# Modulation loads emitted a step ahead, sums stored later, and the backward scan pass re-cut into one chunk per half projection

## The chip, the cores and the metric

The kernel runs on one core of a Trainium2 chip. A core has a matrix engine (TensorE, PE in the profile, with its weight loads shown as PEld), a vector engine (VectorE, DVE), an activation engine (ScalarE, ACT), GpSimd (POOL) and a sync engine (SyncE, SP) whose queue issues nearly all DMA transfers. PSUM is the memory that matmuls write to, SBUF the one that everything else lives in. The metric is the time of one execution on the device, in microseconds (us). All arithmetic is in 32-bit floats.

## The reference

One layer of a diffusion backbone for 256 prompt tokens and 1024 sample tokens of width 1024, which share all weights. A conditioning vector per group gives shift, scale and gate vectors through one large product (the modulation). The mixer has a short gated convolution and a Mamba-2 scan (SSD) that runs over the tokens in chunks of 128, forward and backward. A gated feed-forward block with a 3x3 convolution follows. Cut to what matters here:

```python
mod_lat = (silu(c) @ w_ada + b_ada).reshape(c.shape[0], 1, N_MOD, D_MODEL)   # and mod_ctx from c_ctx
proj = h @ w_in                                     # hc, gb, gc, z, xbc, dtf, dtb
out_a = gb * dwconv1d(gc * hc, w_conv_short)
xbc = silu(dwconv1d(xbc, w_conv_ssd, b_conv_ssd))   # -> xs, bm (B), cm (C)
dt = softplus(dtf + dt_bias)                        # and the same for dtb
# scan, per chunk of 128 positions and head
da = dt * a;  cs = cumsum(da)                       # within the chunk
chunk_states = einsum('bcshn,bhcs,bcshp->bchpn', b_c, exp(cs[-1] - cs), x * dt)
state = exp(cs[-1]) * state + chunk_states          # from chunk to chunk
y = ((C B^T) * exp(cs_l - cs_s)) @ (x * dt) + exp(cs) * (C @ state_at_start)
```

The backward scan is the same over reversed positions. The prompt starts from zero states and returns its final ones; the sample starts from given states.

## The kernel before, in words

Large products are done as three matmuls in a rounded format (`mm3`): the weight tile is split into a high and a low part, and so is the activation. Lines 166, 168 and 170 issue high x high, high x low and low x high. `wload` loads a weight tile of 512 KB into `raw`, ACT rounds it to the high part (line 157), and DVE or GpSimd subtracts to get the low part (`wlo`). A sample projection has 1024 columns and accumulates in an `acc` tile of PSUM, a prompt projection has 256 and uses `pj`.

Between about 70 and 230 us the kernel makes the eight `xbc` tiles of the scan's input (sample and prompt, function `xbc_both`; "the seventh tile" is the one with i = 7, which is made last), and among them small prompt projections and eight modulation steps (`ada_steps`, a generator advanced by `next(mods)`). A modulation step multiplies eight weight tiles `ws` (128 x 512, eight buffers) with the conditioning vectors (line 186: sixteen matmul instructions in the trace, in two groups of four tiles), copies the result to `ss` and transposes it (line 196). `dtstage` and `dtstage2` turn the raw time steps into `dt`, the sums `cs` and decay factors on DVE and ACT, and store `cs` to DRAM in `csdp` (prompt) and `csds` (sample), from where `ssd_pass2` later broadcasts them over the partitions (`bc`).

The scan has two passes. `ssd_pass1` is the backward one: it goes through the chunks from the last to the first (prompt chunks 1 and 0, sample chunks 7 to 1). For each chunk `tok_major` transposes x (line 576, PSUM tile `xt`) and B (line 579, `bt`), ACT copies `bt` to `btok`, DVE scales `xt` to `xd`. `state_step` then forms the products of `btok` and `xd` (line 594, PSUM tile `ad`), and adds them to the decayed state, which DVE (or ACT by a copy, line 600, for the first) writes to `sb`; the state is stored to DRAM (`sbdp`, `sbds`). All of `xt`, `bt` and `ad` come from three PSUM buffers named `sa`. `ssd_pass2` is the forward pass; its `prep` adds masks to the broadcast sums (`wm`) on DVE and takes exponentials on ACT (line 676).

While the scan runs on small matmuls, PE gets long ones from `fillers`: the z projections and the gated-convolution projections of the sample, each in two halves (`next(filler)` runs one half). In pass 1, two chunks were handled for every z projection.

The order on each engine follows the order in which the code emits instructions, as changed by the scheduler of the framework, which may move an instruction past others that it does not depend on; `after(a, b)` asks for a to come behind b. Each engine then works through its list in order and waits where a semaphore says so; so does SP's queue of transfers.

Of the kernel before, what the change touches and what calls it, by code (L numbers as in the profile page):

```python
# [13 lines left out]
P = 128  # L14
# [4 lines left out]
L = 128  # L19
# [36 lines left out]
def body(nc, tc, A):  # L56
    cnt = [0]

    def T(pool, shape, tag, bufs, dt=F32):
        cnt[0] += 1  # L60
        return pool.tile(list(shape), dt, tag=tag, bufs=bufs, name=f"{tag}_{cnt[0]}")
# [12 lines left out]
    dma = nc.sync.dma_start  # L74
# [37 lines left out]
    sc = T(con, [P, KT, 32], "sc", 1)  # L112
# [12 lines left out]
    g_nrm, nrm = open_pool("nrm")  # L125
# [13 lines left out]
    def psa():  # L139
        return T(ps, [P, 512], "sa", 3)  # L140


    wn, w_dma = [0], [None]
# [30 lines left out]

    def ada_steps():

        for e in range(8):
            pt = psa()
            for k0 in (0, 4):
                ws = [T(nrm, [P, 512], "ws", 8) for _ in range(4)]  # L180
                for q, w in enumerate(ws):
                    d = dma(w, A["w_ada"][(k0 + q) * P:(k0 + q + 1) * P, e * 512:(e + 1) * 512])
                    if k0 == q == 0:
                        after(d, w_dma[0])
                for q in (3, 2, 1, 0):
                    mm = nc.tensor.matmul(pt[32 * q:32 * q + 32, :], sc[:, k0 + q, :], ws[q],
                                          start=k0 == 0, stop=k0 == 4, skip_group_check=True,
                                          tile_position=(0, 32 * q))
                    if k0 == 0 and q == 3:
                        after(mm, mid_mm[0])  # L190
            s = T(nrm, [P, 512], "ss", 2)
            act(s, pt, AF.Copy)
            yield
            tp = psa()
            for b in range(4):
                mm = nc.tensor.transpose(tp[:, b * P:(b + 1) * P], s[:, b * P:(b + 1) * P], ident)
                if b == 0:
                    after(mm, mid_mm[0])
            b0 = 16 + e * 4
            V.tensor_reduce(out=mod[:, b0:b0 + 4, :],  # L200
                            in_=tp.rearrange("p (b g v) -> p b v g", b=4, g=4)[:, :, 0:2, :],
                            axis=mybir.AxisListType.X, op=ALU.add)
            tt(mod[:, b0:b0 + 4, :], mod[:, b0:b0 + 4, :],
               smv("bada")[:, b0:b0 + 4].unsqueeze(2).broadcast_to([P, 4, 2]), ALU.add)
        yield
# [8 lines left out]
    def after(a, b):  # L214

        tc.add_manual_dep(a.ins, b.ins.name, mybir.DependencyInfo(
            mybir.DependencyClass.NoSync, mybir.DependencyReason.DATA), reason="table order")
# [35 lines left out]
    for k in range(KT):  # L253
        dma(xs[k], xT[:, k, TP:TT])
        q = T(cv, [P, TS], "cv", 4)
# [61 lines left out]
    for k in range(KT):  # L317
# [23 lines left out]
        q, i = k // 4, k % 4  # L341
# [11 lines left out]
    for name, t0, n, v in (("p", 0, TP, 0), ("s", TP, TS, 1)):  # L353
        s = S()
# [5 lines left out]
    SP, SS = sets  # L360
# [3 lines left out]
    last_mm, mid_mm = [], [None]  # L364
# [6 lines left out]
    def xbc_both(i, order, lo_eng):  # L371

        wh, wl = wload(A["w_in"][16 + i], lo_eng, raw_b())
        for s in order:
            small = s.name == "p"
            pp = pj() if small else pacc()
            outs = [(pp[:, a:b], (lambda k, a=a, b=b: s.hi(k)[:, a:b]), (lambda k, a=a, b=b: s.lo(k)[:, a:b]))
                    for a, b in s.chunks]
            ks = list(range(KT))
            for half in [ks] if small else [ks[0:KT // 2], ks[KT // 2:]]:  # L380
                ends = mm3(outs, wh, wl, KT, half)
                mid_mm[0] = ends[0]
                last_mm.append(ends[-1])
                if half[-1] < KT - 1:
                    yield
            conv_x(s, i, pp[:, 0:s.T], s.xbc[i])
        yield
# [103 lines left out]
    def dtstage(s, d4):  # L491
        n = s.T
        v = T(cv, [40, n], "cv", 4)
        for a, b in s.chunks:
            p2 = psa()
            mm = nc.tensor.matmul(p2[0:40, 0:b - a], sel, d4[:, a:b], start=True, stop=True)
            if a == 0:
                after(mm, last_mm[-1])
            vi = act(v[:, a:b], p2[0:40, 0:b - a], AF.Identity, bias=rows[:, 1:2])
        u = T(cv, [40, n], "cv", 4)  # L500
        stt(u, v, -1.0, v, ALU.mult, ALU.min)
        ex = act(u, u, AF.Exp)
        if s.name == "p":
            after(ex, lnexp_table(vi))
        w = T(cv, [40, n], "cv", 4)
        V.tensor_scalar(out=w, in0=u, scalar1=1.0, scalar2=None, op0=ALU.add)
        lw = T(cv, [40, n], "cv", 4)
        act(lw, w, AF.Ln)
        stt(u, w, -1.0, u, ALU.add, ALU.subtract)
        act(w, lw, AF.Exp, scale=-1.0)  # L510
        tt(u, u, w, ALU.mult)
        tt(lw, lw, u, ALU.subtract)
        stt(v, v, 0.0, lw, ALU.max, ALU.add)
        da = u
        V.tensor_scalar(out=da, in0=v, scalar1=arow, scalar2=None, op0=ALU.mult)
        rm = w
        rm3 = rm.rearrange("p (c l) -> p c l", l=L)
        V.memset(rm, 1.0)
        V.memset(rm3[0:32, :, 0:1], 0.0)
        V.memset(rm3[32:40, :, L - 1:L], 0.0)  # L520
        cs = lw
        V.tensor_tensor_scan(out=cs, data0=rm, data1=da, initial=0.0, op0=ALU.mult, op1=ALU.add)
        V.tensor_tensor_scan(out=cs[32:40, ::-1], data0=rm[32:40, ::-1], data1=da[32:40, ::-1],
                             initial=0.0, op0=ALU.mult, op1=ALU.add)
        for a in range(2):
            for g in range(2):
                r = 32 * a + 4 * g
                dma(s.csd[:, g, a].rearrange("c h l -> h c l"),
                    cs[r:r + 4, :].rearrange("h (c l) -> h c l", l=L))
        return v, u, cs  # L530

    def dtstage2(s, v, u, cs):
        V.tensor_scalar(out=v, in0=v, scalar1=1e-37, scalar2=None, op0=ALU.max)
        act(v, v, AF.Ln)
        tt(v, v, cs, ALU.subtract)
        ce = T(sd, [40, s.nc], f"ce{s.name}", 1)
        cs3 = cs.rearrange("p (c l) -> p c l", l=L)
        V.tensor_copy(ce[0:32, :], cs3[0:32, :, L - 1])
        V.tensor_copy(ce[32:40, :], cs3[32:40, :, 0])
        e2 = u  # L540
        tt(e2.rearrange("p (c l) -> p c l", l=L), v.rearrange("p (c l) -> p c l", l=L),
           ce.unsqueeze(2).broadcast_to([40, s.nc, L]), ALU.add)
        act(e2, e2, AF.Exp)
        return v, e2, ce

    def dttok(s, v, e2, ce):
# [201 lines left out]
    g_nrm, nrm = open_pool("nrm2")  # L748
# [24 lines left out]
    mods = ada_steps()  # L773
    for i, n in zip(range(N_LOOP, 7), (2, 2, 2, 4, 4)):
        for t in range(n):
            next(small)
            if t == 0 and i >= 4:
                next(mods)
        if i == 2:
            dts = dtstage2(SP, *dtstage(SP, d4_p))  # L780
        if i == 4:
            early[0] = False
            bcs = [T(sd, [P, TS], "bcs", 4) for _ in range(4)]
            SS.B, SS.C = bcs[0:2], bcs[2:4]
            SS.xbc += bcs
        both = xbc_both(i, (SS, SP), PG if i < 4 else PV)
        next(both)
        if i > 2:
            next(mods)
        if i == 4:  # L790
            dttok(SS, *dts)
        next(both)
        if i == 2:
            dttok(SP, *dts)
            dts = dtstage(SS, d4_s)
        if i == 3:
            dts = dtstage2(SS, *dts)
        if i == 4:
            after(act(xall, xall, AF.Silu), SS.last_exp)
            for k in range(4):  # L800
                silu_s(k)
        if i >= 4:
            silu_s(i)
        if i == 5:
            act(bcall[:, 0:2], bcall[:, 0:2], AF.Silu)
# [19 lines left out]
    filler = fillers()  # L825
# [7 lines left out]
    def pairs(scan):  # L833
        return [(step, c, copies(c)) for copies, step, c in scan]

    def steps(cps, behind):
        for (step, c, cp), b in zip(cps, behind):
            step(c, cp, b)

    scan = ssd_pass1(SP)  # L840
    both = xbc_both(7, (SP, SS), PV)
    cps = pairs(scan[0:1])
    next(both)
    cps += pairs(scan[1:2])
    next(both)
    act(bcall[:, 2:4], bcall[:, 2:4], AF.Silu)
    silu_s(7)
    steps(cps, (last_mm[-2], last_mm[-1]))
    close_pool(g_ps)
    g_ps, ps = open_pool("ps3", space=PSUM)  # L850
    ph_p[0] = False
    scan = ssd_pass1(SS)
    for i in range(0, len(scan), 2):
        cps = pairs(scan[i:i + 2])
        next(filler)
        mid_mm[0] = last_mm[-1]
        next(filler)
        steps(cps, (last_mm[-2], last_mm[-1]))

    def gate(x, c0, n):  # L860

# [332 lines left out]
    for blk in range(2):  # L1194
        steps = norm2_b_steps() if blk == 0 else final_steps(0, OA)
# [125 lines left out]
```

## Time and profile before

| | |
|---|---|
| time, median of 3 runs | 1573.53 us (1571.55 to 1574.64) |
| the profiled execution's own time | 1575.05 us |
| its span, first to last instruction | 1572.7 us |
| mean granted TensorE clock | 0.990 |
| PE busy | 1524.0 us, 97% of the span |
| DVE busy | 1094.2 us, 70% |
| ACT busy | 653.2 us, 42% |
| HBM traffic | 163.70 MB read, 22.63 MB written |

A row of the timeline reads: start in us, length in us, engine, line of the code, operation, tile written <- tiles read, shape, number of instructions merged; in brackets the idle time of the engine ahead of it and who ended it. Tile names are without their buffer numbers. "SPq" rows are transfers being issued by SP's queue, not their landing. The granted clock is the share of full speed that the clock throttle left to PE.

### The profile page before, as it was taken

The numbers are of one execution on the slowest core, as the hardware profiler recorded it, in microseconds if no ns is written. First come the engines' busy times: TensorE is split into PE (matmuls) and PEld (weight loads), VectorE is DVE, ScalarE is ACT, GpSimd is POOL, SyncE is SP. The second block draws the span as 40 slices with busy tenths as digits, with TensorE's granted clock in tenths as the row PEclk, the third lists the DMA queues.
The fourth block names the chain that finished last, engine by engine and source line by source line (L and its number), as shares of the span: only waits on it lengthen the run. The fifth ranks groups of instructions, "written<-read, shape, count | busy, mean of one in ns | idle before, by whom it ended". The sixth has DMA issues, their size and how long they took to land. (4 is left out here: it accounts for less than half of the span.)

```text
span 1572.7 us, 22526 instructions
## 1 busy us (share of the span) xinstructions
PE 1524.0 (97%) x8722; PEld 1297.4 (82%) x8722; DVE 1094.2 (70%) x1628; ACT 653.2 (42%) x1019; POOL 519.3 (33%) x289
## 2 busy tenths in 40 slices
PE   6999998999999999999999999999999999999997
PEld 2577886787788888888888888888888888888886
DVE  4764354258886448896666597656679878798696
ACT  6444434157786335433322353222344433433333
POOL 0431331111111001434333333333346545455452
PEclk9999999999999999999999999999999999999999
DMA  8445653344434613221222242222243333343321
GB/s 296 157 159 177 216 197 128 110 150 145 141 110 164 254 55 112 82 76 66 78 73 68 66 146 92 73 69 66 95 164 104 92 107 99 101 156 98 94 78 61
DMA packets 90652, 187.79 MB, mean 119 GB/s; under 512 B 9746, under 2 KB 37298, under 8 KB 90546
## 3 DMA queue, kind: packets, MB, share of 16 engines
q1 hardware_dynamic: 84722, 183.22, 34.8%
q10 hardware_dynamic: 5824, 3.15, 0.7%
q8 instruction: 68, 1.11, 0.3%
q14 instruction: 38, 0.31, 0.1%
HBM read 163.70 MB, written 22.63 MB: 118 GB/s over the span
## 5 line engine op out<-in xcount | busy, mean ns | idle before, releaser
L80 DVE SCALAR_TENSOR_TENSOR cc<-acc,sm,cc 128x504 f32<-128x504 f32 (+5 forms) x836 | 545.9, 665 | 111.2 <-ACT cc L1061 52.3
L77 POOL TENSOR_TENSOR wlo<-raw,whi 128x1024 fp32r<-128x1024 f32 (+2 forms) x91 | 214.7, 2359 | 652.3 <-ACT whi L157 608.7
L157 ACT ACTIVATE whi<-raw 128x1024 fp32r<-128x1024 f32 x97 | 102.6, 1057 | 250.1 <-PE acc L168 211.9
L80 DVE SCALAR_TENSOR_TENSOR x<-dn,mod,x 128x288 f32<-128x288 f32 (+2 forms) x176 | 96.1, 547 | 95.2 <-PE dn L170 94.5
L77 POOL TENSOR_TENSOR dlo<-draw,dhi 128x512 fp32r<-128x512 f32 (+1 forms) x88 | 108.9, 1238 | 91.1 <-ACT dhi L1114 91.1
L77 POOL TENSOR_TENSOR wlx<-raw,whx 128x1024 fp32r<-128x1024 f32 (+2 forms) x36 | 83.5, 2320 | 147.2 <-ACT whx L157 131.4
L168 PE MATMUL acc<-ya,whi 128*128 128x512 f32 (+1 forms) x400 | 118.7, 354 | 0.0
L166 PE MATMUL acc<-ya,whi 128*128 128x512 f32 (+1 forms) x400 | 118.7, 354 | 0.0
L170 PE MATMUL acc<-ya,wlo 128*128 128x512 f32 (+1 forms) x400 | 118.6, 354 | 0.0
L170 PE MATMUL acc<-oa,wlo 128*128 128x512 f32 (+1 forms) x400 | 118.5, 354 | 0.0
L168 PE MATMUL acc<-oa,whi 128*128 128x512 f32 (+1 forms) x400 | 118.5, 353 | 0.0
L166 PE MATMUL acc<-oa,whi 128*128 128x512 f32 (+1 forms) x400 | 118.1, 353 | 0.0
L166 PE MATMUL dn<-yb,dhi 128*128 128x288 f32 (+2 forms) x352 | 110.2, 313 | 5.3 <-DVE x L80 4.1
L168 PE MATMUL dn<-yb,dhi 128*128 128x288 f32 (+2 forms) x352 | 109.6, 311 | 1.1 <-POOL yb L77 1.1
L170 PE MATMUL dn<-yb,dlo 128*128 128x288 f32 (+2 forms) x352 | 109.6, 311 | 0.0
L166 PE MATMUL acc<-h,whi 128*128 128x512 f32 x336 | 109.5, 407 | 0.0
L168 PE MATMUL acc<-h,whi 128*128 128x512 f32 x336 | 106.7, 398 | 0.0
L170 PE MATMUL acc<-h,wlo 128*128 128x512 f32 x336 | 105.9, 397 | 0.0
L1114 ACT ACTIVATE dhi<-draw 128x512 fp32r<-128x512 f32 (+1 forms) x88 | 52.9, 602 | 122.5 <-PE dn L168 50.4
L166 PE MATMUL dn<-g,dhi 128*128 128x288 f32 (+2 forms) x304 | 95.1, 313 | 0.2 <-DVE x L80 0.2
L168 PE MATMUL dn<-g,dhi 128*128 128x288 f32 (+2 forms) x304 | 94.8, 312 | 0.3 <-POOL g L77 0.3
L170 PE MATMUL dn<-g,dlo 128*128 128x288 f32 (+2 forms) x304 | 94.8, 312 | 0.0
(336 smaller groups left out, 3566.6 us busy)
## 6 DMA issues: line engine op xcount, KB each, us to landing
raw<-in_w_up SPq DMA_DIRECT2D x88, 512.0 KB, 3.2
ws<-in_w_ada SPq DMA_DIRECT2D x64, 256.0 KB, 4.9
raw<-in_w_in SPq DMA_DIRECT2D x32, 512.0 KB, 4.4
draw<-in_w_down SPq DMA_DIRECT2D x64, 256.0 KB, 2.8
xs<-in_w_ad SPq DMA_DIRECT2D x16, 512.0 KB, 8.4
bc<-csds SPq DMA_DIRECT2D x16, 512.0 KB, 3.4
raw<-in_w_out SPq DMA_DIRECT2D x16, 512.0 KB, 3.3
x<-in_xT SPq DMA_DIRECT2D x8, 640.0 KB, 9.6
```

Of the source, the lines that this page charges most:

```text
L77: (eng or V).tensor_tensor(out=out, in0=a, in1=b, op=op)
L80: V.scalar_tensor_tensor(out=out, in0=a, scalar=s, in1=b, op0=op0, op1=op1)
L157: act(hi, raw, AF.Copy)
L166: nc.tensor.matmul(o, wh[:, k, :], rh(k), start=k == 0, stop=False)
L168: nc.tensor.matmul(o, wh[:, k, :], rl(k), start=False, stop=False)
L170: mm = nc.tensor.matmul(o, wl[:, k, :], rh(k), start=False, stop=k == n - 1)
L1114: act(wh, raw, AF.Copy)
```

## The change

Three edits. The modulation step's eight weight tiles are now requested by a function `load(e)` that is called one step earlier: the loads of step e + 1 are emitted behind the matmuls of step e, and the first ones before the first step, so that there is one more `next(mods)` (at the tile i = 2). The stores of the sums move from the end of `dtstage` to the end of `dtstage2`. In pass 1 the prompt's two chunks are transposed before the seventh tile begins and their products issued between the two halves of its sample part, where the first sample chunk is also transposed; and the loop over sample chunks takes one chunk for each half of a z projection, with the transposes of the next chunk emitted ahead of the half and the products of the present one behind it.

```diff
     def ada_steps():
+        def load(e):
+            ws = [T(nrm, [P, 512], "ws", 8) for _ in range(8)]
+            for k, w in enumerate(ws):
+                dma(w, A["w_ada"][k * P:(k + 1) * P, e * 512:(e + 1) * 512])
+            return ws
+        ws = load(0)
+        yield
         for e in range(8):
             pt = psa()
             for k0 in (0, 4):
-                ws = [T(nrm, [P, 512], "ws", 8) for _ in range(4)]
-                for q, w in enumerate(ws):
-                    d = dma(w, A["w_ada"][(k0 + q) * P:(k0 + q + 1) * P, e * 512:(e + 1) * 512])
-                    if k0 == q == 0:
-                        after(d, w_dma[0])
                 for q in (3, 2, 1, 0):
-                    mm = nc.tensor.matmul(pt[32 * q:32 * q + 32, :], sc[:, k0 + q, :], ws[q],
+                    mm = nc.tensor.matmul(pt[32 * q:32 * q + 32, :], sc[:, k0 + q, :], ws[k0 + q],
...
+            if e < 7:
+                ws = load(e + 1)
             s = T(nrm, [P, 512], "ss", 2)
             act(s, pt, AF.Copy)
             yield
```

```diff
     def dtstage(s, d4):
...
-        for a in range(2):
-            for g in range(2):
-                r = 32 * a + 4 * g
-                dma(s.csd[:, g, a].rearrange("c h l -> h c l"),
-                    cs[r:r + 4, :].rearrange("h (c l) -> h c l", l=L))
         return v, u, cs
     def dtstage2(s, v, u, cs):
...
         act(e2, e2, AF.Exp)
+        for a in range(2):
+            for g in range(2):
+                r = 32 * a + 4 * g
+                dma(s.csd[:, g, a].rearrange("c h l -> h c l"),
+                    cs[r:r + 4, :].rearrange("h (c l) -> h c l", l=L))
         return v, e2, ce
```

```diff
         next(both)
-        if i > 2:
-            next(mods)
+        next(mods)
...
     scan = ssd_pass1(SP)
     both = xbc_both(7, (SP, SS), PV)
+    cps = pairs(scan)
+    next(both)
+    steps(cps, (last_mm[-2], last_mm[-1]))
+    scan = ssd_pass1(SS)
     cps = pairs(scan[0:1])
-    next(both)
-    cps += pairs(scan[1:2])
     next(both)
     act(bcall[:, 2:4], bcall[:, 2:4], AF.Silu)
     silu_s(7)
-    steps(cps, (last_mm[-2], last_mm[-1]))
     close_pool(g_ps)
     g_ps, ps = open_pool("ps3", space=PSUM)
     ph_p[0] = False
-    scan = ssd_pass1(SS)
-    for i in range(0, len(scan), 2):
-        cps = pairs(scan[i:i + 2])
+    for i in range(len(scan)):
+        cps += pairs(scan[i + 1:i + 2])
         next(filler)
         mid_mm[0] = last_mm[-1]
-        next(filler)
-        steps(cps, (last_mm[-2], last_mm[-1]))
+        steps(cps[0:1], (last_mm[-1],))
+        cps = cps[1:]
```

What this does to the order on the engines is seen at three places. Numbers behind tile names are the program's own buffer counts; lines of the changed kernel are a few higher or lower.

First, SP's queue around modulation step 1: `ws` are the step's weight tiles, `csds` the sample's sums, `raw` a weight tile of a projection. Before:

```order
L155 DMA raw_1292<-in_w_in 128x1024
L182 DMA ws_1068<-in_w_ada 128x512
...
L182 DMA ws_1071<-in_w_ada 128x512
L528 DMA csds_565<-cv_820 4x8x128 x4
L182 DMA ws_1080<-in_w_ada 128x512
...
L182 DMA ws_1083<-in_w_ada 128x512
L155 DMA raw_1359<-in_w_in 128x1024
L182 DMA ws_1171<-in_w_ada 128x512
```

Now:

```order
L155 DMA raw_1308<-in_w_in 128x1024
L180 DMA ws_957<-in_w_ada 128x512
...
L180 DMA ws_964<-in_w_ada 128x512
L547 DMA csds_565<-cv_836 4x8x128 x4
L155 DMA raw_1375<-in_w_in 128x1024
L180 DMA ws_1092<-in_w_ada 128x512
```

The four stores of sums have moved behind the second four of step 1's loads. The weight load that follows (`raw_1359`, now `raw_1375`) and step 2's loads (`ws_1171`, now `ws_1092`) stand in the same order as before; so do all later modulation loads.

Second, PE in the seventh tile and at the start of the filler: `sa` tiles written from `xp`/`xs` and `cst` are transposes of x for prompt and sample, those from `bcp`/`bcs` transposes of B, those from `xd` and `btok` the products; `acc_2125` (now `acc_2137`) is the tile's sample part, `acc_2240` the first z projection. Before, from the second half of the tile on:

```order
L576 MATMUL sa_2150<-cst_66,xp_569 128x128 x4
...
L166 MATMUL acc_2125<-h_419,whi_2093 128x512 x2
...
L594 MATMUL sa_2191<-xd_2089,btok_2087 128x256 x2
L594 MATMUL sa_2197<-xd_2160,btok_2158 128x256 x2
L576 MATMUL sa_2210<-cst_66,xs_180 128x128 x4
L579 MATMUL sa_2215<-cst_66,bcs_1128 128x128
L579 MATMUL sa_2215<-cst_66,bcs_1129 128x128
L576 MATMUL sa_2222<-cst_66,xs_180 128x128 x4
...
L166 MATMUL acc_2240<-h_228,whi_2236 128x512 x2
```

Now:

```order
L599 MATMUL sa_2162<-xd_2089,btok_2087 128x256 x2
L599 MATMUL sa_2168<-xd_2101,btok_2099 128x256 x2
L581 MATMUL sa_2177<-cst_66,xs_180 128x128 x4
L584 MATMUL sa_2182<-cst_66,bcs_1144 128x128
...
L166 MATMUL acc_2137<-h_419,whi_2105 128x512 x2
...
L581 MATMUL sa_2222<-cst_66,xs_180 128x128 x4
...
L166 MATMUL acc_2240<-h_228,whi_2236 128x512 x2
...
L599 MATMUL sa_2266<-xd_2187,btok_2185 128x256 x2
```

The products of both prompt chunks and the transposes of sample chunk 7 now stand ahead of the tile's second half, those of chunk 6 alone behind it, and chunk 7's products behind the first half of the z projection. The other prompt chunk's six transposes have moved from between the halves to the prompt part of the tile.

Third, ACT in the same place: `wm` are the masks of pass 2 whose exponentials are taken, `bc` the broadcast sums, `sb` the copy of the first backward state, `btok` the copies of the transposed B. Before:

```order
L676 ACT_TABLE_LOAD
L676 ACTIVATE wm_2601<-wm_2601,tokp_794 128x128
L581 ACTIVATE btok_2158<-sa_2155 128x256
L676 ACTIVATE wm_2601<-wm_2601,tokp_794 128x128 x7
L678 ACTIVATE bc_2576<-bc_2576 128x1024
L676 ACTIVATE wm_2615<-wm_2615,tokp_794 128x128 x5
L157 ACTIVATE whi_2332<-raw_2330 128x1024
L391 ACTIVATE bcs_1131<-acc_2125,sm_63 128x1024
L600 ACTIVATE sb_2194<-sa_2191 128x512
```

Now:

```order
L681 ACT_TABLE_LOAD
L681 ACTIVATE wm_2601<-wm_2601,tokp_810 128x128 x3
L605 ACTIVATE sb_2165<-sa_2162 128x512
L681 ACTIVATE wm_2601<-wm_2601,tokp_810 128x128 x4
L586 ACTIVATE btok_2185<-sa_2182 128x256
L681 ACTIVATE wm_2601<-wm_2601,tokp_810 128x128
L683 ACTIVATE bc_2576<-bc_2576 128x1024
```

The copy of the state has moved ahead of most of the exponentials, and behind three of them. `sa_2182` takes the buffer of `sa_2162`, and so waits for that copy.

## The prediction

> **What bounds the kernel now.** I read the busy shares first, then the table of 25 us stretches, the waits of PE, and then PE's timeline where it stands still.
>
> ```profile
> span 1572.7 us, 22526 instructions
> PE 1524.0 (97%) x8722; PEld 1297.4 (82%) x8722; DVE 1094.2 (70%) x1628; ACT 653.2 (42%) x1019; POOL 519.3 (33%) x289
> ...
> PE   6999998999999999999999999999999999999997
> ```
>
> PE works in all but 48.7 us of the span, and in the last row, its busy share in 40 slices in tenths, 9 stands nearly everywhere. A change that removes no matmul, as this one, can gain only from that idle time and from time in which PE's clock is held down. The stretches (columns: PE, PEld, DVE, ACT, POOL busy, then the granted clock, DMA share, GB/s) show both where the change lies, between 100 and 330 us:
>
> ```profile
> 125.00:150.00 25.00, 21.27 (x124) 14.52 (x123) 9.36 (x18) 11.58 (x17) 4.77 (x2) 0.89 0.72 258
> 150.00:175.00 25.00, 25.00 (x174) 21.78 (x174) 7.28 (x12) 12.55 (x17) 5.88 (x3) 0.98 0.45 159
> 250.00:275.00 25.00, 18.16 (x79) 14.70 (x79) 11.24 (x13) 8.93 (x14) 4.72 (x2) 0.86 0.28 88
> 275.00:300.00 25.00, 23.75 (x112) 19.49 (x111) 6.53 (x8) 3.12 (x5) 2.37 (x1) 1.00 0.31 101
> ```
>
> ```profile
> PE sa L579 <- DVE sb L77: 5.0, 1, 5.0
> PE sa L186 <- DMA ws<-in_w_ada: 3.7, 3, 2.0
> PE sa L576 <- DVE xd L77: 2.5, 2, 1.2
> PE sa L579 <- ACT btok L581: 0.6, 1, 0.6
> ```
>
> Four waits, then: one on the modulation's weights (3.7 us), three on the backward pass's PSUM buffers "sa" (8.1 us). Whatever PE gains before 330 us should reach the end, for PE is busy through every later slice too.
>
> **Backward pass: what it costs now.** PE's timeline:
>
> ```profile
> 241.53 0.60 PE L576 MATMUL sa<-cst,xp 128*128 128x128 f32 x4
> ...
> 247.69 1.89 PE L594 MATMUL sa<-xd,btok 128*128 128x256 f32 x8
> 249.41 0.60 PE L576 MATMUL sa<-cst,xs 128*128 128x128 f32 x4
> 255.04 0.69 PE L579 MATMUL sa<-cst,bcs 128*128 128x128 f32 x2 [5.03 <-DVE sb L77]
> ...
> 257.14 0.69 PE L579 MATMUL sa<-cst,bcs 128*128 128x128 f32 x2 [0.56 <-ACT btok L581]
> ...
> 258.48 1.05 PE L168 MATMUL acc<-h,whi 128*128 128x512 f32 x2
> ...
> 260.77 0.63 PE L168 MATMUL acc<-h,whi 128*128 128x512 f32 x2
> ...
> 271.67 0.60 PE L576 MATMUL sa<-cst,xs 128*128 128x128 f32 x4
> ...
> 272.24 0.71 PE L166 MATMUL acc<-h,whi 128*128 128x512 f32 x2
> ...
> 274.44 0.66 PE L576 MATMUL sa<-cst,xs 128*128 128x128 f32 x4 [1.25 <-DVE xd L77]
> ...
> 289.96 0.66 PE L576 MATMUL sa<-cst,xs 128*128 128x128 f32 x4 [1.25 <-DVE xd L77]
> ```
>
> Idle: 5.03 + 0.56 + 2 x 1.25 = 8.1 us. Clock: the granted 0.86 over 250 to 275 means 0.14 x 25 = 3.5 us of clock missing, that is 7.0 us at half rate. The pairs of matmuls take 1.05 us at 258.48 and 0.63 at 260.77, so it ended near 260.4 and began near 253.4. Of these 7.0 us PE idled 1.6 (to 255.04) and 0.56; the remaining 4.8 us at half rate lost 2.4. Together 10.5 us.
>
> [...]
>
> **Backward pass: what the change makes of it.** The wait of 5.03 us comes from three "sa" buffers being asked for six tiles in one place, while DVE, which must free them, is busy with the convolution and masks of the seventh tile. The new order puts the prompt's products (L594) between the two sample halves of the seventh tile, so that the sum they feed is read before the half ends 5.5 us later, and in the filler halves one chunk's ad, xt and bt (three tiles, three buffers) stand between two halves. The conflict inside one group is gone; between groups DVE and ACT have a half projection.
>
> ```profile
> 271.73 2.05 DVE L77 TENSOR_TENSOR sb<-sb,decs 128x512 f32<-128x512 f32 x1
> 273.70 0.68 DVE L77 TENSOR_TENSOR xd<-sa,toks 128x512 f32<-128x512 f32 x1
> ```
>
> A chunk costs DVE one product, one sum, one xd: at the worst 2.05 + 0.68 + 0.68 = 3.4 us, less than a half projection: the second one of the seventh tile takes 5.6, from 241.53 plus 0.57 for six transposes (271.67 to 272.24) to 247.69. I take the 2 x 1.25 as gone.
>
> What is late next is ACT. In the new order the copy of the first state (sa to sb, L605 after, L600 before) stands behind three exponentials of the masks, and these wait for the broadcast of the prompt's sums. The transposes of sample chunk 7's B (sa_2182) need the buffer that this copy frees, and the second sample half is queued behind them on PE.
>
> ```profile
> 237.22 1.95 SPq L664 DMA_DIRECT2D bc<-csdp  x4
> ...
> 242.85 2.38 DVE L77 TENSOR_TENSOR wm<-bc,sm 128x1024 f32<-128x1024 f32 x2 [5.13 <-DMA bc<-csdp]
> ...
> 244.11 0.40 ACT L676 ACTIVATE wm<-wm,tokp 128x128 f32<-128x128 f32 x1 [4.37 <-DVE wm L77]
> ...
> 244.69 2.15 ACT L676 ACTIVATE wm<-wm,tokp 128x128 f32<-128x128 f32 x7
> ...
> 251.17 0.59 ACT L600 ACTIVATE sb<-sa 128x512 f32<-128x512 f32 x1
> ```
>
> ACT gets there at 244.11 + 3 x 0.31 + 0.59 = 245.6. PE: the first half ended at 241.53; six transposes moved ahead of it (0.57) and a hand-over from DVE (0.1, estimated) make 242.2; four products (1.72, 247.69 to 249.41) and four transposes (0.43) bring it to 244.4. New wait: 1.2 us. Its bounds: nothing, if the broadcast lands 1.2 us sooner (second store and weight load have changed places on SP's queue, so it may by 0.3), and 5.6 us if it lands 4.4 us later. The row itself, 5.6 us from issue to use, says 1.2.
>
> Small change: two more places where long matmuls follow short ones, 0.1 us each (0.71 at 272.24 against 0.63 at 260.77), and 0.2 estimated for hand-overs: 0.4. Loads of weights that now stand behind state stores on SP need their data a whole projection (11 us) later, so nothing. Sum: 10.5 - 1.2 - 0.4 = 8.9 us gained.
>
> **Modulation.** The loads look new, but on SP's queue they hardly move: the four loads of step 1's second half pass the four stores of sums.
>
> ```profile
> 126.40 1.06 PE L186 MATMUL sa<-ws,sc 128*32 128x512 f32 x8
> 129.13 1.06 PE L186 MATMUL sa<-ws,sc 128*32 128x512 f32 x8 [1.35 <-DMA ws<-in_w_ada]
> ...
> 133.91 0.63 PE L170 MATMUL acc<-h,wlo 128*128 128x512 f32 x2
> ...
> 139.60 1.06 PE L186 MATMUL sa<-ws,sc 128*32 128x512 f32 x8 [0.43 <-DMA ws<-in_w_ada]
> 142.62 1.07 PE L186 MATMUL sa<-ws,sc 128*32 128x512 f32 x8 [1.95 <-DMA ws<-in_w_ada]
> ```
>
> ```profile
> 113.72 1.78 SPq L182 DMA_DIRECT2D ws<-in_w_ada  x4
> 118.79 3.48 SPq L528 DMA_DIRECT2D csds<-cv  x4
> 122.37 1.78 SPq L182 DMA_DIRECT2D ws<-in_w_ada  x4
> 132.54 0.33 SPq L155 DMA_DIRECT2D raw<-in_w_in  x1
> 132.97 3.93 SPq L182 DMA_DIRECT2D ws<-in_w_ada  x8
> ```
>
> ```profile
> 129.53 2.95 DVE L77 TENSOR_TENSOR wlo<-raw,whi 128x1024 fp32r<-128x1024 f32 x1
> ```
>
> The 1.35 us goes: the loads no longer stand behind stores that wait for DVE's scan until 118.79, and are issued by 113.72 + 2 x 1.78 = 117.3, some 10 us ahead of use. But step 2's eight loads stand, before and after, behind a weight load that waits until DVE has split the previous tile (129.53 + 2.95 = 132.48, issue 132.54). Nothing in that chain is PE's: DVE comes from its own work on the sample's time steps. The weights land when they did, PE is there sooner and waits the longer: it resumes at 142.62 either way (and the L170 matmul at 133.91, which needs that same split, could not start before 132.5). Gain: 0. The four stores still go when DVE lets them, at 118.79. Bounds: 1.35 gained if step 2's loads land sooner after all; 0.7 lost if the longer idle brings the half rate of the stretch at 125 forward onto the group at 142.62 (1.07 us, in the ratio 1.05 to 0.63).
>
> [...]
>
> I stay at 8.9, since the group at 142.62 still ran at full rate (1.07 against 1.06 at 126.40), with 2.38 us of idle time just ahead of it.
>
> **Rivals.** (1) The modulation's wait does go, and its clock with it. Idle 3.73 us; clock missing 0.11 x 25 + 0.02 x 25 = 3.25 us; together 7.0: 1557.6. For it: step 1's loads do come early enough. Against it: the row at 132.54. Half of it, the 1.35 alone, would give 1563.2.
>
> (2) ACT's block is larger. If the broadcast lands 3.4 us later than the row says, the new wait is 4.6 us, about the length that took the clock before; the gain is 8.9 - 3.4 - 2.4 = 3.1: 1570.4. For it: the copy has moved from behind the masks' second half to inside the first, and four broadcasts and a weight load share the DMA. Against it: these were there before.
>
> (3) Slower. The three buffers make every one of the seven groups in the filler wait, because each now takes all three. This decides when a wait per group exceeds 8.9 / 7 = 1.3 us, that is, when DVE needs 5.6 + 1.3 = 6.9 us to free them; at 2 us each PE loses 14: 1578.6. Against it: 3.4 us at the worst in the rows above. For it: the present waits of 1.25 us are of just this kind.
>
> (4) The wait only changes its name: ACT's block reaches its upper bound of 5.6 us, which costs the clock again, and the gain is 8.9 - 4.4 - 2.4 = 2.1: 1571.4, no change that can be told. For and against it stands what was said of (2), and it needs the broadcast 4.4 us late.
>
> **How the numbers follow.** Forecast 0.60; rival 1 0.12, rival 2 0.14, rival 3 0.07, rival 4 0.07. The profiled execution took 1575.05 us (span 1572.7 and 2.35 around it), 1.5 above the median of 1573.53. For it the forecast is 1566.1, a span of 1563.8; for the median 1573.53 - 8.9 = 1564.6. Range 1559.5 to 1568.5: downward past the half of rival 1, upward past the middle of rival 2, leaving under 0.2 outside. About 0.2% (3.1 us) is what a measurement of this kernel can tell from no change; the three runs spread over 3.1 us. Faster: forecast, rival 1 and nearly all of rival 2, 0.85; same 0.08; slower 0.07.
>
> **What the profile after would show.** Right: no wait on DVE sb of 5 us; a wait of 1 to 1.5 us at chunk 7's B transposes, put down to ACT; granted clock 1.00 for 250 to 275; no wait at 129, but 1.8 and 2 us in front of step 2's two groups; PE's idle in 225 to 300 down from 8.1 to near 1.5. Wrong: a granted clock under 0.95 after 240; waits for DVE in each filler half; step 2's weights landing well ahead of 142.

## The result, and the profile after

The changed kernel takes 1562.13 us (median of 7 runs, 1558.24 to 1566.7) against 1571.55 (7 runs, 1568.02 to 1574.64) for the kernel before in the same sessions: ratio 0.994, 95% interval 0.9919 to 0.9961, or 9.4 us less. The forecast was 8.9 us less. The profiled execution took 1562.46 us. First its page:

```profile
span 1560.4 us, 22524 instructions
...
PE 1519.2 (97%) x8722; PEld 1294.2 (83%) x8722; DVE 1095.0 (70%) x1628; ACT 652.9 (42%) x1019; POOL 518.8 (33%) x289
```

PE idles 41.2 us, 7.5 less than before. Then the stretches (granted clock in the third column from the end):

```profile
125.00:150.00 25.00, 22.10 (x107) 15.07 (x107) 7.48 (x12) 10.04 (x14) 4.75 (x2) 0.80 0.65 231
225.00:250.00 25.00, 23.72 (x145) 20.77 (x144) 14.96 (x20) 13.91 (x30) 2.83 (x2) 1.00 0.50 179
250.00:275.00 25.00, 25.00 (x120) 20.72 (x119) 9.74 (x12) 6.31 (x9) 4.47 (x2) 1.00 0.31 95
275.00:300.00 25.00, 25.00 (x118) 20.81 (x117) 8.16 (x9) 4.71 (x6) 4.81 (x2) 1.00 0.46 137
```

The backward pass, from 240 on, has no half rate left and no idle time but 1.28 us; the modulation's stretch has a lower clock than before, 0.80 against 0.89. PE's waits there:

```profile
PE sa L189 <- DMA ws<-in_w_ada: 2.7, 2, 2.0
...
PE sa L584 <- ACT sb L605: 1.3, 1, 1.3
...
PE acc L170 <- DVE wlo L77: 0.2, 1, 0.2
```

The waits on DVE's sb and xd are gone, and the filler groups have none. To see where the time went, the same instruction is looked up in both timelines. Of the changed kernel:

```profile
109.21 1.92 PE L189 MATMUL sa<-ws,sc 128*32 128x512 f32 x16
...
229.04 0.60 PE L581 MATMUL sa<-cst,xp 128*128 128x128 f32 x4
...
302.59 0.60 PE L581 MATMUL sa<-cst,xp 128*128 128x128 f32 x4
```

Of the kernel before:

```profile
112.65 1.92 PE L186 MATMUL sa<-ws,sc 128*32 128x512 f32 x16
...
232.39 0.60 PE L576 MATMUL sa<-cst,xp 128*128 128x128 f32 x4
...
315.24 0.60 PE L576 MATMUL sa<-cst,xp 128*128 128x128 f32 x4
```

The first row is modulation step 0, the second the first transposes inside the seventh tile, the third the first transposes of pass 2. Up to step 0 the profiled execution is 3.44 us ahead. From there to the seventh tile the two differ by 0.09 (119.74 against 119.83), in the backward pass by 9.30 (82.85 against 73.55), and behind it by 0.35 the other way (1257.46 against 1257.81). So 12.3 us between the spans, of which the change made 9.3, all in the backward pass. The 3.44 us ahead of it lie where the change touches nothing. The stretch 25 to 50 us, before and then after, has most of it in the clock:

```profile
25.00:50.00 25.00, 21.68 (x129) 11.86 (x127) 18.95 (x30) 11.53 (x22) 8.06 (x6) 0.80 0.56 200
```

```profile
25.00:50.00 25.00, 20.72 (x147) 10.95 (x143) 22.16 (x36) 13.71 (x24) 7.92 (x7) 1.00 0.73 249
```

0.80 against 1.00 is 5 us of missing clock in the one execution and none in the other. This is what the comparison of medians averages out.

### The profile page after: what moved, and what is told of

Same layout as the page of the kernel before. It is cut to its first block, busy times and chain, and to the rows that moved or that the text cites. A ratio compares the mean times of both kernels' runs of the same rounds, so it can differ in the third digit from the quotient of the medians.

```text
span 1560.4 us, 22524 instructions
## 1 busy us (share of the span) xinstructions
PE 1519.2 (97%) x8722; PEld 1294.2 (83%) x8722; DVE 1095.0 (70%) x1628; ACT 652.9 (42%) x1019; POOL 518.8 (33%) x289
```

## Experiments

Each kernel was compared with runs of the kernel before on the same chip; ratios are to those, with 95% intervals.

**The modulation and store edits alone** (pass 1 in the third block of the change undone; the extra `next(mods)` stays):

```diff
-    for i in range(len(scan)):
-        cps += pairs(scan[i + 1:i + 2])
...
+    for i in range(0, len(scan), 2):
+        cps = pairs(scan[i:i + 2])
```

> The kernel before with the modulation edit and the later stores, pass 1 as before. My theory (the weights of step 2 stand behind a weight load that waits for DVE): no change of time, ratio 0.998 to 1.002; the wait of 1.35 us before step 1's second group is gone and the waits before step 2's two groups grow by as much, to 3.5 to 4 us in sum; PE leaves the small products behind step 2 within 0.5 us of where it left them before, counted from the start of the sixteen matmuls of step 0. The rival (loading ahead removes the wait and its clock): 4 to 7 us faster, ratio 0.9955 to 0.9975, full granted clock from 125 to 175 us.

Measured: 1568.54 us (12 runs), ratio 0.9993 [0.9978, 1.0008]. PE's timeline at step 2:

```profile
136.78 1.07 PE L189 MATMUL sa<-ws,sc 128*32 128x512 f32 x8 [1.96 <-DMA ws<-in_w_ada]
139.38 1.94 PE L189 MATMUL sa<-ws,sc 128*32 128x512 f32 x8 [1.53 <-DMA ws<-in_w_ada]
```

No wait is left at step 1, and 3.5 us at step 2. The loss moved and the time stayed. PE left step 2's products 31.7 us behind step 0's start (139.38 + 1.94 - 109.61) against 31.0 before, 0.7 later where 0.5 at most was expected: the second group ran at half rate here, 1.94 us against 1.07.

**The backward pass alone** (the first two blocks and the extra `next(mods)` undone, so that the steps load four tiles at a time again):

```diff
-        ws = load(0)
-        yield
...
+                ws = [T(nrm, [P, 512], "ws", 8) for _ in range(4)]
```

> The kernel before with the new pass 1 alone, modulation and stores as before. My theory: all of the gain is here, 8.5 to 9.5 us, ratio 0.9935 to 0.9955, and a wait of 1.0 to 1.5 us for ACT's copy of the first state. The rival (part of the gain comes from the loads): 4 to 6 us, ratio 0.996 to 0.9975.

Measured: 1563.18 us (6 runs), ratio 0.9953 [0.9935, 0.9971], 7.4 us less. That is under the 8.5 to 9.5 us expected and above the rival's 4 to 6; the ratio is within the expected range, and the interval contains the whole change's 0.994. The new wait was a little longer than expected:

```profile
PE sa L579 <- ACT sb L600: 1.8, 1, 1.8
```

**Step 2's loads ahead of the weight load.** If the loads wait only because a load that waits for DVE stands ahead of them on SP, changing the two places must free them. The changed kernel, with `ws_dma[e]` the last load of step e:

```diff
         wh, wl = wload(A["w_in"][m], lo_eng, raw_b())
+        if s.name == "p" and m == 8:
+            after(w_dma[0], ws_dma[2])
```

> The changed kernel, in which the weight load that waits for DVE (the prompt's second projection of the first gated tile) is queued on SP behind step 2's eight loads and not ahead of them. My theory: these loads are issued about 5 us sooner (near 124 instead of 129.6 in the profiled execution), both waits before step 2's groups (2.05 and 0.62 us) go, and with them the half rate behind: 5 to 7 us faster than the changed kernel, ratio to the kernel before 0.989 to 0.992. The rival (the DMA itself is what limits, eight loads landing at their own pace whatever stands ahead of them): waits of 2 us or more stay, within 2 us of the changed kernel, ratio near 0.994.

Measured: 1554.49 us (1554.36 to 1555.43, 5 runs), ratio 0.9897 [0.9879, 0.9915]. Its SP queue, PE and the stretch:

```profile
124.66 3.69 SPq L180 DMA_DIRECT2D ws<-in_w_ada  x8
129.75 0.80 SPq L155 DMA_DIRECT2D raw<-in_w_in  x2
```

```profile
134.96 1.92 PE L189 MATMUL sa<-ws,sc 128*32 128x512 f32 x16
```

```profile
125.00:150.00 25.00, 24.77 (x167) 19.87 (x160) 10.95 (x17) 15.28 (x20) 6.49 (x3) 1.00 0.69 231
```

The loads go some 5 us sooner, step 2 runs as one piece, the clock stays at 1.00. In the same comparison the kernel of the next experiment, which differs from the changed one by under a microsecond, took 1562.13: the move is worth about 7 us, and it beats both kernels.

**ACT's copy first.** The changed kernel, with the copy of the first state (`cp0`) asked ahead of the masks' exponentials (`ex`):

```diff
+                    if s.name == "p" and u.c == 0:
+                        after(ex, cp0[0])
```

> The changed kernel with ACT's copy of the first backward state put ahead of the masks' exponentials. My theory (the copy stands behind exponentials that wait for the broadcast of the sums): the wait of 1.28 us before chunk 7's B transposes goes, and nothing takes its place: 1.3 us faster than the changed kernel, ratio 0.993. The rival (the copy would wait for something else, or the exponentials that are now later hold up the copies of B behind them): the wait changes its releaser, 0 us, ratio 0.994.

Measured: 1562.13 us (6 runs), ratio 0.9945 [0.9926, 0.9964]. The wait at chunk 7's B is gone; two small ones appear behind the tile:

```profile
257.81 0.66 PE L581 MATMUL sa<-cst,xs 128*128 128x128 f32 x4 [0.29 <-DVE xd L77]
...
258.78 0.44 PE L584 MATMUL sa<-cst,bcs 128*128 128x128 f32 x2 [0.31 <-ACT btok L586]
```

Expected was that nothing takes its place. Net 0.7 us (1.28 - 0.29 - 0.31) in the trace, too little for the times to show. That the wait was ACT's order is shown; that it costs time is not.

**The tile part alone**: the prompt's products inside the seventh tile, and behind it two chunks for each z projection as before.

```diff
     steps(cps, (last_mm[-2], last_mm[-1]))
-    scan = ssd_pass1(SS)
-    cps = pairs(scan[0:1])
     next(both)
...
+    scan = ssd_pass1(SS)
-    for i in range(len(scan)):
-        cps += pairs(scan[i + 1:i + 2])
+    for i in range(0, len(scan), 2):
+        cps = pairs(scan[i:i + 2])
```

> The modulation and store edits, and of the backward pass the prompt's products inside the seventh tile alone; behind the tile two sample chunks are handled for every z projection as before. The forecast's theory: the pile-up of six tiles for three buffers is what cost 5.03 us of wait, 0.56 behind it and 2.4 of clock, so all 8.0 go; the two waits of 1.25 us on DVE's xd stay, and a third of the kind may come at the first pair. The copy of the first state is long done when chunk 7 asks for its buffer, so no wait on it. Gain 7 to 8 us, 1563.5 to 1564.5, ratio 0.995; clock 1.00 from 250 to 275. Rival (what counts is one chunk per half, and the order in the tile only moves the conflict behind it): a wait of 3 us or more stands at the first pair of sample chunks, the clock is lost there, and the gain is under 3 us (ratio over 0.998).

Measured: 1571.16 us (10 runs), ratio 1.0008 [0.9992, 1.0025]. No gain: my expectation missed, the rival held. The wait has only moved to the first pair of sample chunks (PE, then DVE and ACT):

```profile
252.47 0.69 PE L584 MATMUL sa<-cst,bcs 128*128 128x128 f32 x2 [5.34 <-DVE xd L77]
```

```profile
244.80 1.22 DVE L77 TENSOR_TENSOR bc<-bc,bcp 128x1024 f32<-128x1024 f32 x1 [0.26 <-ACT bc L683]
...
249.22 2.59 DVE L80 SCALAR_TENSOR_TENSOR bcs<-acc,sm,bcs 128x1023 f32<-128x1023 f32 x2
251.73 1.28 DVE L77 TENSOR_TENSOR xd<-sa,toks 128x512 f32<-128x512 f32 x2
```

```profile
247.00 1.04 ACT L683 ACTIVATE bc<-bc 128x1024 f32<-128x1024 f32 x1
247.95 1.19 ACT L396 ACTIVATE bcs<-acc,sm 128x1024 f32<-128x1024 f32 x1
```

Four tiles asked of three buffers are enough. The fourth waits until DVE has read the first, and DVE's xd stands behind the products of pass 2's masks and the tile's convolution taps; the start of the taps on ACT (247.95) stands behind ACT's sixteen mask exponentials and ends at 249.14, just before DVE takes the taps up.

**The loop part alone**: one chunk for each half projection, the prompt's products behind the tile as before.

```diff
-    cps = pairs(scan)
+    cps = pairs(scan[0:1])
     next(both)
-    steps(cps, (last_mm[-2], last_mm[-1]))
-    scan = ssd_pass1(SS)
-    cps = pairs(scan[0:1])
+    cps += pairs(scan[1:2])
     next(both)
...
+    steps(cps, (last_mm[-2], last_mm[-1]))
+    scan = ssd_pass1(SS)
+    cps = pairs(scan[0:1])
```

> The modulation and store edits, and of the backward pass the loop of one chunk per half projection alone; the prompt's products stand behind the seventh tile as before. The forecast's theory: the prompt's two products and the transposes of chunks 7 and 6 still want six tiles of three buffers in one place, so the wait of 5 us and the clock of 0.86 stay, and only the 2 x 1.25 us go: gain 2 to 2.5, ratio 0.9985. Rival: one chunk per half also spreads the first pile-up, the 5 us wait falls under 2, the clock goes to 1.00 and the gain is over 6 us (ratio under 0.996).

Measured: 1567.56 us (10 runs), ratio 0.9987 [0.9971, 1.0002], as expected 0.9985, though the interval touches no change. The large wait stays and the two of 1.25 are gone:

```profile
PE sa L584 <- DVE sb L77: 5.4, 1, 5.4
```

So neither part removes the large wait: 0 and about 2 us apart, 7.4 to 9.3 together.

**DVE's list.** Is it the count of buffers or DVE's list that PE waits for? The tile part alone, with the pair's transposes emitted ahead of the seventh tile's convolution, so that xd stands ahead of the taps:

```diff
+            if i == 7 and not small:
+                yield
             conv_x(s, i, pp[:, 0:s.T], s.xbc[i])
...
     next(both)
+    scan = ssd_pass1(SS)
+    cps = pairs(scan[0:2])
+    next(both)
...
-    scan = ssd_pass1(SS)
     for i in range(0, len(scan), 2):
-        cps = pairs(scan[i:i + 2])
+        if i:
+            cps = pairs(scan[i:i + 2])
```

> The kernel with the tile part alone, with one thing moved: the transposes of sample chunks 7 and 6 are emitted ahead of the seventh tile's convolution, so that DVE's two xd stand ahead of its two convolution taps (2.59 us in the tile-only trace) and behind the masks' products. It asks what held the buffer that PE waited 5.34 us for. Theory 1 (DVE's list: the xd stood behind the masks' products and the taps): xd goes at 249.3 instead of 251.7, the wait falls from 5.34 to about 2.9 us, the time falls by 2.4 to 4 us (ratio 0.997 to 0.999), the clock may still be lost. Theory 2 (three buffers for four tiles, whatever DVE does): the wait stays above 4.5 us and the ratio at 1.000 or above.

And the same with the exponentials of the masks behind the tile's convolution start on ACT (`id7`), which moves the masks' products on DVE behind xd too:

```diff
+                    if s.name == "p" and u.c == 0:
+                        after(ex, id7[0])
```

> The same, and the exponentials of the prompt's masks on ACT asked to come behind the seventh tile's convolution start on ACT, which takes the masks' products on DVE behind the two xd as well. Theory 1: DVE reaches the first xd as soon as its transposes are there, the wait falls to 0.5 to 1 us, no half rate follows, and with the 2 x 1.25 us left the gain on the kernel before is 6 to 7.5 us (ratio 0.9955 to 0.997); the masks are late by some us but pass 2 needs them only some 50 us later. Theory 2 (buffers): the wait stays above 4.5 us. Theory 3: the wait goes, but the later masks cost as much further on (two more table loads of 1.28 us on ACT stand in its list): ratio 0.999 or above.

Measured: 1567.99 us, ratio 0.9992 [0.9976, 1.0007], and 1565.32 us, ratio 0.9964 [0.9951, 0.9978] (10 runs each). PE, DVE and ACT with the taps moved:

```profile
252.69 0.69 PE L586 MATMUL sa<-cst,bcs 128*128 128x128 f32 x2 [2.43 <-ACT btok L588]
...
253.90 1.22 PE L166 MATMUL acc<-h,whi 128*128 128x512 f32 x2 [0.53 <-ACT btok L588]
```

```profile
251.31 1.23 DVE L77 TENSOR_TENSOR bc<-bc,bcp 128x1024 f32<-128x1024 f32 x1 [0.25 <-ACT bc L685]
252.45 1.28 DVE L77 TENSOR_TENSOR xd<-sa,toks 128x512 f32<-128x512 f32 x2
```

```profile
247.90 2.44 ACT L683 ACTIVATE wm<-wm,tokp 128x128 f32<-128x128 f32 x8
...
252.27 0.36 ACT L588 ACTIVATE btok<-sa 128x256 f32<-128x256 f32 x1
```

With both moved:

```profile
249.34 0.74 PE L166 MATMUL acc<-h,whi 128*128 128x512 f32 x2 [0.40 <-ACT btok L590]
```

```profile
247.75 1.35 DVE L77 TENSOR_TENSOR xd<-sa,toks 128x512 f32<-128x512 f32 x2 [0.20 <-PE sa L585]
```

5.34, then 2.43 + 0.53, then 0.40 us, with the same four tiles and three buffers. With the taps moved it is ACT that ends the wait: its copy btok is done at 252.27 + 0.36 = 252.63, behind eight exponentials, and PE starts at 252.69, before DVE's first xd ends (252.45 + 0.68). So the length came as theory 1 said, and the engine did not. The wait is the length of what stands ahead of the instruction that frees the buffer, xd on DVE or the copies on ACT. No run had a fourth buffer, so what the count alone is worth is not shown. With both moved the kernel gains 5.7 us on the kernel before (0.0036 of 1570.81), a little under the 6 to 7.5 expected and with the ratio in its range, without any of the change's loop part. With the taps alone moved the wait shrank as expected, but the time fell by only 2.5 us on the tile part alone (1.0008 to 0.9992), which the intervals don't tell from nothing; a clock of 0.86 is left between 250 and 275.

**Both moves, and the first one again.** The changed kernel with the loads' and the copy's move:

```diff
+        if s.name == "p" and m == 8:
+            after(w_dma[0], ws_dma[2])
...
+                        after(ex, cp0[0])
```

> The changed kernel with both moves: the weight load behind step 2's loads, and ACT's copy of the first state ahead of the exponentials. Theory 1: the wait of 1.28 us at chunk 7's B goes and 0.6 us of small waits on xd and btok come back as with the copy alone, so 0.7 us below the weight load's move alone: 1553.8, ratio 0.9893, within 1.5 us from run to run. Theory 2: with the clock at full rate throughout, the delayed exponentials push pass 2's masks and the time is the same or up to 1 us more (1554.5 to 1555.5). Theory 3: the 1.28 us had been covered elsewhere and nothing changes at all.

Measured: 1555.06 us (1552.87 to 1557.7, 6 runs), ratio 0.9915 [0.9896, 0.9934]. Theory 1's 0.9893 and its spread of 1.5 us are both missed; nothing beyond the loads' move can be told.

> The changed kernel with the weight load behind step 2's loads once more, on the chip of the last comparisons' kind. Its five times lay within 1.1 us, those with the ACT copy moved as well within 4.8. [...] Theory 2 (the narrow spread was chance, or that chip's): 4 us or more between its runs, at a ratio of 0.989 to 0.992.

Measured, the same edit as with the loads' move above: 1555.63 us (1554.25 to 1556.82, 4 runs), ratio 0.9909 [0.9888, 0.9931]. The gain repeats. The spread of 2.6 us lies under the 4 us of theory 2; runs of the kernel before spread over 7.6 there.

**The loads' move without the new backward pass** (the modulation and store edits, pass 1 as in the kernel before, and the two added lines):

```diff
+        if s.name == "p" and m == 8:
+            after(w_dma[0], ws_dma[2])
```

> The modulation and store edits, the backward pass as in the kernel before, and the weight load of prompt w_in tile 8 put behind step 2's loads. It asks whether the gain of that move and the narrow spread of its times belong to the modulation alone. Theory 1 (they do): the waits in front of step 2 and the half rate there go, 6 to 8 us below the modulation edits alone: 1562 to 1565, ratio 0.994 to 0.997, and its runs agree within 2 us although the wait of 5 us in the backward pass is still there. [...] Theory 3 (the gain came only together with the new backward pass): ratio above 0.998.

Measured: 1564.24 us (1562.14 to 1567.22, 10 runs), ratio 0.997 [0.9957, 0.9984]. Against the modulation edits alone (0.9993) that is about 3.6 us, half of the 6 to 8 expected, though the time and the ratio lie at the upper end of theory 1's ranges; the spread is 5 us, not within theory 1's 2.

Why about 7 us with the new backward pass and 3.6 without it? The traces, read at the places of the section on the result (one execution each, in us), don't show this difference:

| kernel | step 0 to seventh tile | seventh tile to pass 2 |
|---|---|---|
| before | 119.7 | 82.9 |
| changed | 119.8 | 73.6 |
| modulation and stores alone | 120.3 | 82.7 |
| backward pass alone | 116.3 | 74.1 |
| tile part alone | 119.3 | 82.6 |
| loop part alone | 116.2 | 79.6 |
| changed, loads' move | 112.6 | 73.7 |
| loads' move, old backward pass | 112.6 | 82.4 |

In the first stretch the move takes 7.2 us off the changed kernel and 7.7 off the modulation edits alone; the second stretch stays as it was. The table also shows that the first stretch scatters without the move: the loop part's execution has the changed kernel's modulation and its two waits at step 2, but both groups ran at full rate, and the stretch took 3.6 us less:

```profile
135.21 1.07 PE L189 MATMUL sa<-ws,sc 128*32 128x512 f32 x8 [1.61 <-DMA ws<-in_w_ada]
137.99 1.07 PE L189 MATMUL sa<-ws,sc 128*32 128x512 f32 x8 [1.72 <-DMA ws<-in_w_ada]
```

The twelve times of the modulation edits alone run from 1566.1 to 1573.8 us, at mean clocks of 0.995 down to 0.989. That the medians differ by less because some of these executions kept the clock at step 2 is likely; without a trace of each it is not shown.

## Why the prediction was right, and where only its sum was

**Backward pass, predicted 8.9 us, measured 9.30.** The terms: the 8.1 us idle and 2.4 us of clock went as booked. That the clock was at half rate for some 7 us, which the prediction worked out from 0.86 over 25 us, the trace before shows: granted clock 0.50 from 253.6 to 260.3. In the changed kernel's trace it is 1.00 from 229 to 260. ACT's wait was put at 1.2 us and is 1.28 (that it is so close is partly luck: the same wait was 1.4 and 2.2 us in the two traces of the loads' move):

```profile
240.74 0.60 PE L581 MATMUL sa<-cst,xs 128*128 128x128 f32 x4
...
242.62 0.44 PE L584 MATMUL sa<-cst,bcs 128*128 128x128 f32 x2 [1.28 <-ACT sb L605]
```

```profile
241.10 0.99 ACT L681 ACTIVATE wm<-wm,tokp 128x128 f32<-128x128 f32 x3 [3.87 <-DVE wm L77]
241.99 0.57 ACT L605 ACTIVATE sb<-sa 128x512 f32<-128x512 f32 x1
```

The three exponentials and the copy end at 242.56; the forecast's 245.6, less the 3.35 us by which this execution is ahead at the seventh tile, is 242.25. The two small costs of 0.4 us, of which 0.2 for hand-overs had no row behind it, are not to be seen: 10.5 - 1.28 is 9.22. The medians' 9.4 has an interval of 6.1 to 12.7 us, so that it came within 0.5 us of the forecast is luck too; the direction and the rough size are not.

The cause was told too simply. The prediction's step, three "sa" buffers being asked for six tiles in one place, would have let the tile part take the 5 us, and the expectation built on it missed by all of its 7 to 8 us. Six or four tiles, the wait lasts until the engine has come through what the scheduler put ahead of the instruction that frees the buffer. In the kernel before this is DVE's sum at 254.31, which stands behind both convolution taps, the first of which waited 2.28 us for ACT:

```profile
251.32 1.28 DVE L80 SCALAR_TENSOR_TENSOR bcs<-acc,sm,bcs 128x1023 f32<-128x1023 f32 x1 [2.28 <-ACT bcs L391]
...
254.31 0.68 DVE L77 TENSOR_TENSOR sb<-sa,sb 128x512 f32<-128x512 f32 x1
```

The change wins because chunk 7's transposes now stand between the halves, ahead of that pile (DVE scales them at 243.21, ahead of the taps at 250.61), and because only two tiles are asked for behind the tile. Each part alone left a wait of over 5 us; the sum was right since they were booked as one. That DVE is busy with "convolution and masks" was said; that the length of this list sets the wait, and that ACT's list does as much, was not.

**Modulation, predicted 0, measured 0.1 lost in this pair of traces.** Right as to the queue: the weight load waits for DVE's split, and step 2's loads are issued right behind it.

```profile
110.28 3.68 SPq L180 DMA_DIRECT2D ws<-in_w_ada  x8
...
129.12 0.36 SPq L155 DMA_DIRECT2D raw<-in_w_in  x1
129.57 3.92 SPq L180 DMA_DIRECT2D ws<-in_w_ada  x8
```

```profile
129.11 0.73 PE L170 MATMUL acc<-h,wlo 128*128 128x512 f32 x2 [0.23 <-DVE wlo L77]
...
136.45 1.93 PE L189 MATMUL sa<-ws,sc 128*32 128x512 f32 x8 [2.05 <-DMA ws<-in_w_ada]
139.01 1.94 PE L189 MATMUL sa<-ws,sc 128*32 128x512 f32 x8 [0.62 <-DMA ws<-in_w_ada]
...
146.66 0.63 PE L166 MATMUL acc<-h,whi 128*128 128x512 f32 x2
```

Of the two waits, 1.8 and 2 us forecast, the first is 2.05 and the second 0.62. Both groups now run at half rate (1.93 against 1.06 before, granted clock 0.50 from 136.5 to 146.5), and the first one's longer run takes the place of the second one's wait: the weights landed when they did before (139.01 + 3.44 is 142.45, against 142.62). The same 55 us of the program, before and after, each from 12.65 us ahead of step 0's row:

```profile
100.00:155.00 55.00, 51.27 (x301) 38.91 (x301) 29.95 (x41) 23.30 (x32) 12.63 (x5) 0.94 0.46 159
```

```profile
96.56:151.56 55.00, 52.10 (x300) 38.56 (x300) 30.37 (x40) 23.20 (x32) 12.60 (x5) 0.91 0.46 159
```

Idle time fell by 0.83 us and PE was busy 0.83 longer with the same work, at a clock of 0.91 instead of 0.94. The half rate set in one wait sooner (in the trace before the granted clock is 0.50 only from 144.5 on, behind the second group at 142.62); that this would cost 0.7 us, the prediction's lower bound, the trace does not bear out. Waits at the same place cost the clock here (2.05 and 0.62 us, 0.80 over 125 to 150 us) and left it at 1.00 in the loop part's trace (1.61 and 1.72 us, the same stretch). So the 0.1 is luck of two executions, which can differ by 3.6 us in this stretch; the forecast of 0 rests on the twelve runs of the modulation edits alone, 0.9993 [0.9978, 1.0008].

**The rivals.** (1) The wait did not go: the row at 129.57 held, and the kernel with the two loads exchanged shows that it was this queue: about 7 us (7.1 from 119.7 to 112.6 in the traces), the price that rival 1 had named (7.0). (2) and (4) needed the broadcast 3.4 or 4.4 us late; the masks' additions started at 239.84, which is 0.3 us later than 242.85 - 3.35:

```profile
239.84 2.42 DVE L77 TENSOR_TENSOR wm<-bc,sm 128x1024 f32<-128x1024 f32 x2 [4.63 <-DMA bc<-csdp]
```

(3) No filler group waits: DVE's 3.4 us for a chunk, an estimate from the rows before, stayed under a half projection (5.6 us, 248.98 to 254.57 in the trace after).

## What to carry to other kernels

A wait for a buffer was here as long as the list ahead of the instruction that frees it (5.34, then 2.43 + 0.53, then 0.40 us with the same tiles): look at what the scheduler put there before counting buffers, and be ready for two halves of a cure to do little alone (0 and about 2 us, 7.4 to 9.3 together). Requesting a load earlier in the code gained nothing (ratio 0.9993) where it stood in SP's queue behind a load that waited for an engine; find the one that waits and exchange the two (about 7 us). Compare traces by looking up the same instruction at several places, since one execution can be ahead of another before the change begins (3.44 us here, against 9.30 that the change made).

## What the runs showed of the hardware

Runs of one kernel scatter by 8 us: the changed one had spans of 1556.5, 1560.3 and 1564.9 us at mean granted clocks of 0.997, 0.993 and 0.990. The same start-up code had 0.80 in one trace and 1.00 in another for the stretch 25 to 50 us (shown above), and 0.86 or 0.93 in four others. What decides it, no run here shows. Half rate (a granted clock of 0.50) set in behind a wait of 2.05 us with one of 0.23 us some 7 us ahead of it, while 1.61 and 1.72 us at the same place in the loop part's trace, and the 1.28 us at chunk 7's B, left the clock at 1.00. With the taps moved, two waits on the same weights, 3.1 us together and neither over 1.6, came with a clock of 0.80 from 125 to 150 us, against 1.00 beside the loop part's 3.3. So in these traces the length of the waits alone does not tell whether the clock is lost. Whether short spread is a property of a kernel without such waits stays open: nine runs of the loads' move lie within 2.6 us, six with the copy's move added within 4.8.
